# A block product in place of four seventh products, and a new order of products, in a Strassen-like matmul with RMS norm

## The chip, the cores and the metric

The kernel runs on one core of one Trainium2 chip. Its metric is the device time of one execution in microseconds (us). Of the kernel before there are three runs: 220.96, 221.03 and 221.49 us, median 221.03 us. A profile of one execution belongs to it.

The engines' names below: TensorE (PE) multiplies matrices, PEld is its loading of weights; VectorE (DVE), ScalarE (ACT) and GpSimd (POOL) work on elements; SyncE (SP) and POOL issue DMA transfers.

## The reference

```python
def reference(a, b, gamma, eps):           # all float32; a, b: 2048 x 2048
    x = np.matmul(a, b)
    rms = np.sqrt(np.mean(x ** 2, axis=-1, keepdims=True) + eps)
    return (gamma * x / rms).astype(np.float32)
```

Each output row needs the whole row of `x` for its root mean square before it can be scaled and stored.

## The kernel before

**Tiles.** The 16 blocks of 128 rows of `a` are rows 0 to 15 here. `b` stays in SBUF as bfloat16, in tiles `raw[j][kp]`: `j` is the left or right half of N (1024 columns), `kp` one of eight pairs of 128 rows of K. Rows 0 to 3 and the loading of `b` come first (lines 432 to 557). From there on two rows make a group `g`: group 2 is rows 4 and 5, group 7 rows 14 and 15. A group is worked in two halves, `j` = 0 (left) and `j` = 1 (right), in `group_half` (line 582); the last group has its own `last_group` (line 705).

**Seven products.** In a half, the 2 x 2 blocks of `a` (two rows by even and odd blocks of K) and of `b` (the two blocks of K in a pair by two runs of 512 columns) are multiplied by Strassen's scheme: seven products, numbered 1 to 7, in place of eight. One product is 8 matmuls, one for each `kp`, into one PSUM bank of 128 x 512 (`product`, line 289). The sums of `b` are made while it is loaded; products 2, 5, 6 and 7 read `raw` itself, and 7 reads `b_quarter(j, kp, 1, 0)`. The sums of `a` are made by `a_sums` (line 254) on VectorE, for each group during the right half of the group before. Products 3 and 4 need no sum of `a`.

**A half.** `group_half` issues products 2, 5, 1, 4, 3, 7, 6. ScalarE empties the first bank into a tile (line 597); VectorE adds the second to it (601), subtracts that from product 1 (605). Products 4 and 3 then accumulate onto the first two banks, and ScalarE copies them to the output tiles `x21` and `x12` (608, 613) and squares them for the norm (303). VectorE combines them to `x11` and `x22` (610, 615, 619, 624). Seven PSUM banks are handed out in turn by `new_bank` (line 391); a bank given again waits for its last reader.

**Work in between.** `hooks_of` (line 634) lists, for places 0 to 7 between the products, what else is issued there. In a left half (`j` = 0) these are, for the two rows of the next group: the row norm of the loaded block (line 219, ScalarE), a power-of-two factor from it (`row_factor`, VectorE), the rescaled block in float16 (line 242, ScalarE) and its transposing DMA (line 195, SP); for the rows of the group before: the root (`take_rms`, line 332) and the scaling with gamma (line 370, VectorE) and the stores (SP). In a right half they are the second row's scaling (`finish`), the sums of the next group and the loads of the rows after (`load_after`, POOL, which waits until `x22` of the left half is written). Squares of the last two tiles of a half are put off to the next half's start (`last_squares`, line 573).

**What sets the order.** The kernel schedules by hand (`tc.manual_schedule()`): each engine's instructions run in the order in which the code issues them, and what connects engines are waits for the data or for a buffer to be free. Output tiles are eight `x_slot` buffers of 128 x 1024, four to a group; blocks of `a` are loaded into two `a32` buffers.

Of the kernel before, what the change touches and what calls it, by code (L numbers as in the profile page):

```python
# [9 lines left out]
BF16 = mybir.dt.bfloat16  # L10
# [7 lines left out]
def kernel(  # L18
# [61 lines left out]
    def a16_slot(mb):  # L80
        if mb == HB:
            return gamma_sb[:, 0:HALF].bitcast(FP16)
        flat = head_at.rearrange("p t r m -> p (t r m)").bitcast(FP16)
        return flat[:, (2 + mb % 2) * K:(3 + mb % 2) * K]

    s_sum = {s: consts.tile([P, KP, P], FP16, name=f"s_{s}") for s in (1, 2, 5, 6, 7)}

    def at(mb):
        return (at_even, at_odd)[(mb // 2) % 2][:, mb % 2]
# [159 lines left out]
        return at(2 * g + r)[:, c::2, :]  # L249

    def sum_of(g, s):
        return s_sum[s].bitcast(BF16) if g < G0 else s_sum[s]

    def a_sums(g, which, lo=0, hi=KP):
        a11, a12, a21, a22 = (quarter(g, r, c) for r in range(2) for c in range(2))
        terms = {1: (a11, a22, ALU.add), 2: (a21, a22, ALU.add), 5: (a11, a12, ALU.add),
                 6: (a21, a11, ALU.subtract), 7: (a12, a22, ALU.subtract)}
        for s in which:
            x, y, op = terms[s]
            nc.vector.tensor_tensor(out=sum_of(g, s)[:, lo:hi, :], in0=x[:, lo:hi, :],  # L260
                                    in1=y[:, lo:hi, :], op=op)
# [32 lines left out]


    x_half = {}
    n_x = [0]

    def square(mb, src):
        c = n_sq[mb]  # L300
# [5 lines left out]
    def square_half(mb, h):  # L306
# [3 lines left out]
        nc.scalar.activation(out=sq, in_=x_tile(mb, h), func=ACTF.Square,  # L310
                             scale=inv_sqrt_n, accum_out=msq[mb][:, c:c + 1])

    def x_tile(mb, h):


        if (mb, h) not in x_half:
            n = n_x[0]
            n_x[0] += 1
            if n < 8:
                slot = n  # L320
            else:
                g = n // 4
                slot = ((0, 4, 1, 5), (0, 1, 4, 5))[g // 2 % 2 == 0][n % 4] + 2 * (g % 2)
            x_half[mb, h] = x_slot[slot]
        return x_half[mb, h]

    def x_chunk(mb, c):
# [219 lines left out]
    nc.scalar.copy(out=x12, in_=pair[5])  # L547
    p6 = new_bank()
    product(PAIR, 1, 6, p6, within={5 + g: [lambda g=g: turn(HB + 1, g)] for g in range(2)})
    a_sums(G0, (5,))  # L550
    for g in range(2):
        take_transposed(HB + 1, g, turned[HB + 1, g], nc.vector.tensor_copy)
    square_half(0, 1)
    square_half(1, 1)
    a_sums(G0, (2,))
    take_rms(0)
    a_sums(G0, (1,))

    def pair_sub():
        nc.vector.tensor_tensor(out=x22, in0=pair[1], in1=x22, op=ALU.subtract)  # L560
# [21 lines left out]
    def group_half(g, j, hooks):  # L582
        ra, rb = 2 * g, 2 * g + 1
        c1, c2 = 2 * j, 2 * j + 1

        def at_hook(n):
            for work in hooks.get(n, ()):
                work()

        x11, x12, x21, x22 = (x_chunk(ra, c1), x_chunk(ra, c2), x_chunk(rb, c1), x_chunk(rb, c2))  # L590
        first = (g, j) == (G0, 0)
        c, t = spare if first else (x22, x22)
        at_hook(0)
        p2, p5 = new_bank(), new_bank()
        one, two = ((5, p5), (2, p2)) if first else ((2, p2), (5, p5))
        product(g, j, *one)
        nc.scalar.copy(out=c, in_=one[1])  # L597
        last_squares()
        at_hook(1)
        product(g, j, *two)  # L600
        nc.vector.tensor_tensor(out=t, in0=two[1], in1=c, op=ALU.add)
        at_hook(2)
        p1 = new_bank()
        product(g, j, 1, p1)
        nc.vector.tensor_tensor(out=t, in0=p1, in1=t, op=ALU.subtract)
        at_hook(3)
        product(g, j, 4, p2, start=False)
        nc.scalar.copy(out=x21, in_=p2)
        square(rb, x21)
        nc.vector.tensor_tensor(out=x11, in0=t, in1=x21, op=ALU.add)  # L610
        at_hook(4)
        product(g, j, 3, p5, start=False)
        nc.scalar.copy(out=x12, in_=p5)  # L613
        square(ra, x12)
        nc.vector.tensor_tensor(out=t, in0=t, in1=x12, op=ALU.add)  # L615
        at_hook(5)
        p7 = new_bank()
        product(g, j, 7, p7)
        nc.vector.tensor_tensor(out=x11, in0=p7, in1=x11, op=ALU.add)
        late.append((ra, x11))  # L620
        at_hook(6)
        p6 = new_bank()
        product(g, j, 6, p6)
        nc.vector.tensor_tensor(out=x22, in0=p6, in1=t, op=ALU.add)  # L624
        late.append((rb, x22))
        at_hook(7)

    def load_after(g, mb):

# [4 lines left out]
    def hooks_of(g, j):  # L634


        hooks = {n: [] for n in range(8)}
        nxt = 2 * g + 2

        def hook(n, work, *args):  # L640
            hooks[n].append(lambda: work(*args))

        def apply(mb):
            row_apply(mb)
            transpose_dma(mb)

        more = g + 1 < NG
        if j == 0:
            if g == G0:
                hook(0, finish, 0, (1,))  # L650
                hook(1, row_norm, nxt)
                hook(1, take_rms, 1)
                hook(2, pair_sub)
                hook(2, row_factor, nxt)
                hook(2, apply, nxt)
                hook(2, row_norm, nxt + 1)
                hook(2, pair_sums)
                hook(2, a_sums, g, (7, 6))
                hook(2, finish, 0, (0,))
                hook(2, finish, 1, (1,))  # L660
                hook(2, row_factor, nxt + 1)
                hook(2, pair_ends)
                hook(2, scale, 1, (0,))
                hook(4, apply, nxt + 1)
                hook(4, store, 1, (0,))
                hook(7, late.insert, 0, (r2, None))
            else:
                done = [2 * g - 2, 2 * g - 1]
                if g == G0 + 1:
                    done.insert(0, r3)  # L670
                else:
                    hook(1, row_norm, nxt)
                for mb in done:
                    hook(1, take_rms, mb)
                hook(2, row_factor, nxt)
                hook(2, apply, nxt)
                if g == G0 + 1:
                    hook(2, finish, r3)
                hook(2, row_norm, nxt + 1)
                hook(3, scale, 2 * g - 2)  # L680
                hook(3, row_factor, nxt + 1)
                hook(4, apply, nxt + 1)
                hook(4, store, 2 * g - 2)
        else:
            if g == G0:
                hook(1, take_rms, r2)
                hook(1, square_half, r3, 1)
                hook(2, finish, r2, (1, 0))
            else:
                hook(2, finish, 2 * g - 1)  # L690
            if more:
                hook(3, a_sums, g + 1, (2, 5, 1))
                hook(6, a_sums, g + 1, (7,))
                hook(7, a_sums, g + 1, (6,))
            if g + 2 < NG:
                hook(0, load_after, g, nxt + 2)
                if g == G0:
                    hook(2, wait_for, x_slot[HB + r2][:, 0:1])
                    hook(2, load_block, nxt + 3)
                    hook(5, row_norm, nxt + 2)  # L700
                else:
                    hook(0, load_block, nxt + 3)
        return hooks

    def last_group():
# [33 lines left out]

        p4 = []  # L740
        for j in range(2):
            p5, p1 = new_bank(), new_bank()
            p4.append(new_bank())
            product(g, j, 5, p5)
            nc.scalar.copy(out=t[j], in_=p5)
            last_squares()
            product(g, j, 1, p1)
            add(t[j], p1, t[j], ALU.subtract)
            if j == 0:
                finish(2 * g - 2)  # L750
            product(g, j, 4, p4[j])
            nc.scalar.copy(out=x21[j], in_=p4[j])
            add(x11[j], t[j], x21[j])
            if j == 0:
                finish(2 * g - 1)
            product(g, j, 3, p5, start=False)
            nc.scalar.copy(out=x12[j], in_=p5)
            square(ra, x12[j])
            add(t[j], x11[j], x12[j])
            p7 = new_bank()  # L760
            product(g, j, 7, p7)
            add(x11[j], p7, x11[j])
            square(ra, x11[j])
            if j == 0:
                product(g, j, 2, p4[j], start=False)
                nc.scalar.copy(out=x21[j], in_=p4[j])
                square(rb, x21[j])
                seed = p7
                add(seed, t[j], x21[j], ALU.subtract)
                pre_a = partial(ra)  # L770
                add(xa, xa, gam_left, ALU.mult)
                add(x21[j], x21[j], gam[0], ALU.mult)
        rms_a = root(msq[ra][:, NCH - 1:NCH], plus(pre_a, ra, 2))
        product(g, 1, 2, p4[1], start=False)
        halves = [slice(0, CH // 2), slice(CH // 2, CH)]
        half = [bank[:, 0:CH // 2] for bank in (p1, p7)]
        for bank, col in zip(half, halves):
            add(bank, t[1][:, col], p4[1][:, col], ALU.subtract)
        r_a = inverse(rms_a)
# [75 lines left out]
```

## Time and profile before

| what | us |
|---|---|
| median of three runs | 221.03 |
| span of the profiled execution (first to last instruction) | 219.1 |
| TensorE busy | 209.2 |
| VectorE busy | 165.9 |
| ScalarE busy | 127.0 |
| GpSimd busy | 36.4 |
| end of the last matmul in the span | 212.23 |

The span is what the profile shows of one execution; the device time also holds what lies around it. Busy time counts an engine's own work, not its waits. A matmul of 512 columns is listed with 379 ns, but matmuls overlap: in a row they start about 216 ns apart. The same holds in a smaller way for VectorE and ScalarE: an instruction's listed duration is somewhat longer than the distance to the next one's start.

Where the prediction speaks of windows, these are stretches of the span with the busy time of PE, PEld, DVE, ACT and POOL in this order, then the granted clock of TensorE, the busy share of the DMA engines and GB/s.

### The profile page before, as it was taken

Reading aid. Unit: us, or ns where it says so; the run is one execution under the profiler, and the core shown is the slowest. Engines: PE = TensorE matmul, PEld = TensorE weight load, DVE = VectorE, ACT = ScalarE, POOL = GpSimd, SP = SyncE. Lnnn points to the kernel's source line nnn. Section 1 sums busy time; section 2 is a strip of 40 time slices with the busy share of each in tenths; the row PEclk is TensorE's granted clock in tenths of the full one; section 3 lists DMA queues with packets and bytes.
Section 4 is the critical chain, followed back from the end, with each engine's and each line's share of the span. In section 5 each row is a group of like instructions: output and inputs, shape, how many; then the busy total and the mean of one; then the engine's idle time right before and its main releaser. Section 6 shows DMA issues by size and latency. Waiting matters only on the chain.

```text
span 219.1 us, 3041 instructions
## 1 busy us (share of the span) xinstructions
PE 209.2 (95%) x1032; PEld 97.7 (45%) x1032; DVE 165.9 (76%) x326; ACT 127.0 (58%) x263; POOL 36.4 (17%) x75
## 2 busy tenths in 40 slices
PE   7799999999999999999999999999999999999970
PEld 3344544444455444444444444444444444444440
DVE  1128899999989998969696639946795759787771
ACT  2110002930599898588945996289747996334471
POOL 7554443433020002200110002000200000000040
PEclk9999999999999999999999999999999999999997
DMA  7999999999929698946799149955699259145045
GB/s 156 168 202 206 204 206 209 212 208 228 407 77 330 243 276 218 349 188 165 212 320 399 64 88 271 350 244 96 160 298 400 37 106 361 79 167 219 1 170 215
DMA packets 36720, 46.60 MB, mean 213 GB/s; under 512 B 22240, under 2 KB 26336, under 8 KB 35424
## 3 DMA queue, kind: packets, MB, share of 16 engines
q0 software_dynamic: 10608, 23.86, 44.1%
q1 hardware_dynamic: 25824, 22.29, 33.7%
q10 hardware_dynamic: 272, 0.26, 0.3%
q8 instruction: 8, 0.13, 0.2%
q14 instruction: 8, 0.07, 0.1%
HBM read 34.60 MB, written 16.78 MB: 234 GB/s over the span
## 4 chain that ended last, share of the span: by engine, by line
PE 92%; DMA 3%; ACT 1%; POOL 1%; issue 1%; DVE 0%; ACTq 0%; POOLq 0%
PE acc L285 71%; PE acc L388 16%; DMA early<-in_a_dram 3%; PE tbank L419 2%; PE tbank L168 2%; PE acc L800 1%; POOL b L102 0%; PE acc L185 0%; PE tbank L185 0%; ACT a L738 0%; DVE head_at L173 0%; ACTq L850 0%; ACT sq L803 0%; ACT rms L352 0%; POOL t_left masks.py:199 0%
## 5 line engine op out<-in xcount | busy, mean ns | idle before, releaser
L285 PE MATMUL acc<-b,s 128*128 128x512 bf16 x408 | 93.3, 379 | 0.0
L285 PEld LDWEIGHTS <-s 128*128 128x128 f16 (+1 forms) x512 | 50.0, 98 | 59.6 <-DVE s L260 0.2
L388 PE MATMUL acc<-b,head_at 128*128 128x512 bf16 x176 | 43.0, 379 | 1.2 <-DMA b<-in_b_dram 0.8
L303 ACT ACTIVATE sq<-x 128x512 bf16<-128x512 f32 x53 | 33.4, 630 | 6.9 <-DVE x L731 3.0
L370 DVE SCALAR_TENSOR_TENSOR x<-x,r,gamma_sb 128x1024 f32<-128x1024 f32 x28 | 34.9, 1282 | 0.7
L219 ACT ACTIVATE sq<-a 128x1024 bf16<-128x1024 f32 x24 | 25.3, 1054 | 3.2 <-DMA a<-in_a_dram 2.5
L388 PEld LDWEIGHTS <-head_at 128*128 128x128 bf16 x176 | 16.9, 97 | 20.4 <-issue 1.3
L242 ACT ACTIVATE head_at<-a,s 128x2048 f16<-128x2048 f32 x10 | 20.0, 1996 | 3.3 <-DVE s L229 3.3
L102 POOL DMA_DIRECT2D b<-in_b_dram x32 | 17.2, 541 | 20.6 <-DMA b<-in_b_dram 14.2
L430 ACT COPY x<-acc 128x512 f32<-128x512 f32 x5 | 2.9, 582 | 24.6 <-PE acc L388 24.6
L285 PEld LDWEIGHTS <-head_at 128*128 128x128 f16 (+1 forms) x112 | 10.9, 98 | 13.2
L285 PE MATMUL acc<-early,head_at 128*128 128x512 bf16 x64 | 14.5, 379 | 0.0
L285 PEld LDWEIGHTS <-at_even 128*128 128x128 f16 x96 | 9.4, 98 | 11.3
L285 PE MATMUL acc<-early,s 128*128 128x512 bf16 x56 | 14.2, 379 | 0.0
L260 DVE TENSOR_TENSOR s<-head_at 128x1024 f16<-128x1024 f16 (+5 forms) x22 | 13.4, 635 | 0.1
L615 DVE TENSOR_TENSOR x<-x,x 128x512 f32<-128x512 f32 x9 | 6.2, 693 | 8.8 <-ACT x L613 8.3
L127 POOL COPY pace<-x 128x1 f32<-128x1 f32 x4 | 1.7, 413 | 66.2 <-DVE x L624 64.9
L597 ACT COPY x<-acc 128x512 f32<-128x512 f32 x9 | 5.2, 573 | 11.5 <-PE acc L285 11.5
L173 DVE COPY head_at<-tbank 128x1024 bf16<-128x1024 bf16 x7 | 4.8, 692 | 8.6 <-PE tbank L168 8.5
L285 PE MATMUL acc<-t_left,s 128*128 128x512 bf16 x48 | 11.3, 379 | 0.0
L783 POOL TENSOR_SCALAR x<-x,r 128x512 f32<-128x512 f32 x1 | 2.7, 2657 | 51.2 <-DVE r L346 51.2
L276 DVE TENSOR_TENSOR b<-b 128x1024 bf16<-128x1024 bf16 x16 | 10.8, 686 | 0.2
(112 smaller groups left out, 238.0 us busy)
## 6 DMA issues: line engine op xcount, KB each, us to landing
out_dram<-x SPq DMA_DIRECT2D x29, 512.0 KB, 3.7
a<-in_a_dram POOLq DMA_DIRECT2D x10, 1024.0 KB, 9.0
b<-in_b_dram POOLq DMA_DIRECT2D x32, 256.0 KB, 10.0
a<-in_a_dram POOLq DMA_DIRECT2D x4, 512.0 KB, 9.8
early<-in_a_dram POOLq DMA_DIRECT2D x7, 256.0 KB, 10.0
gamma_sb<-in_gamma_dram POOLq DMA_DIRECT2D x2, 512.0 KB, 8.4
out_dram<-x SPq DMA_DIRECT2D x3, 256.0 KB, 2.6
out_dram<-a SPq DMA_DIRECT2D x1, 768.0 KB, 3.3
```

What stands on the lines that cost most here:

```text
L102: nc.gpsimd.dma_start(out=raw[j][kp][:, t, :], in_=b[lo:lo + P, j * HALF:(j + 1) * HALF])
L173: nc.vector.tensor_copy(out=head_at[:, 2 * kp:2 * kp + 2, :, :], in_=view)
L219: nc.scalar.activation(out=junk, in_=a32[mb][:, h * HALF:(h + 1) * HALF], func=ACTF.Square, scale=2.0 ** -8, accum_out=n2[:, h:h + 1])
L242: nc.scalar.activation(out=a16[mb], in_=a32.pop(mb), func=ACTF.Copy, scale=factor.pop(mb))
L260: nc.vector.tensor_tensor(out=sum_of(g, s)[:, lo:hi, :], in0=x[:, lo:hi, :], in1=y[:, lo:hi, :], op=op)
L276: nc.vector.tensor_tensor(out=flat[:, 1:3, :], in0=flat[:, 1:3, :], in1=flat[:, 0::3, :], op=ALU.add)
L285: nc.tensor.matmul(bank, lhsT[:, kp, :], rhs, start=(start and kp == 0), stop=(kp == KP - 1), skip_group_check=not start)
L303: nc.scalar.activation(out=sq[:, 0:CH], in_=src, func=ACTF.Square, scale=inv_sqrt_n, accum_out=msq[mb][:, c:c + 1])
L370: nc.vector.scalar_tensor_tensor(out=x, in0=x, scalar=inverse_of[mb], in1=gamma_sb[:, h * HALF:(h + 1) * HALF], op0=ALU.mult, op1=ALU.mult)
L388: nc.tensor.matmul(bank, head_at[:, kt, r, :], head_rhs(c, kt), start=(kt == 0), stop=(kt == KT - 1))
L597: nc.scalar.copy(out=c, in_=one[1])
L615: nc.vector.tensor_tensor(out=t, in0=t, in1=x12, op=ALU.add)
```

## The change

Two things change for the groups from 2 on.

*Order.* Products are issued as 3, 4, 1, 5, 2, 7, 6; 5 accumulates onto 3's bank and 2 onto 4's. The sums are rewritten to fit. In groups 4 to 7 product 7 is left out of the half.

*Product 7 of two groups at once.* Groups 4 and 5, and groups 6 and 7, are pairs. The product 7 of both groups and both halves is a 2 x 2 block product: `y` (the two groups' sum 7, each cut in two along K) times `z` (`b_quarter(j, kp, 1, 0)`, two halves of N by two halves of `kp`). It is made by seven block products of 4 matmuls each, 28 matmuls, where four times 8 stood. `z_sums` makes differences of `z` (VectorE, 128 x 512 bf16), 12 of them once during group 4 and 4 in each pair; `y_sums` makes four sums of `y` in each pair (VectorE, 128 x 512 f16). `sevenths` issues the parts: `one` ahead of product 6 of the first group's right half, `two` behind it, `three` behind product 3 of the second group's left half. ScalarE copies a bank into another bank (`seed`), so that a part accumulates onto both. The results go into `x11` of both groups; the second group's `x11` is written before that group starts.

With it go: the second group's sums 1, 5, 2, 6 are made in its own left half, since the block product uses those buffers; the sums of `b` and `a` share buffers (`z_store`, `s_both`, `y_sum`); the blocks of `a` from row 6 on are rescaled to float16 in place in their `a32` buffer; the output tiles' slots are given by a table; the second group of a pair has its rows finished in reversed order.

```diff
+    s_both = consts.tile([P, 2, KP, P], FP16, name="s_both")
+    s_sum |= {2: s_both[:, 0], 5: s_both[:, 1]}
...
+        return a32[mb].bitcast(FP16)[:, 0:K]
...
         at_hook(0)
+        p3, p4 = new_bank(), new_bank()
+        product(g, j, 3, p3)
+        nc.scalar.copy(out=c, in_=p3)
         last_squares()
         at_hook(1)
+        product(g, j, 4, p4)
+        add(t, p4, c)
         at_hook(2)
         p1 = new_bank()
         product(g, j, 1, p1)
+        add(t, p1, t)
+        if second:
+            add(x11, x11, t)
         at_hook(3)
+        product(g, j, 5, p3, start=False)
+        nc.scalar.copy(out=x12, in_=p3)
+        square(ra, x12)
+        add(x11, x11 if second else t, x12, ALU.subtract)
+        if second:
+            late.append((ra, x11))
+        at_hook(4)
+        product(g, j, 2, p4, start=False)
+        nc.scalar.copy(out=x21, in_=p4)
         square(rb, x21)
+        add(t, t, x21, ALU.subtract)
         at_hook(5)
+        if g < FIRST_PAIR:
+            p7 = new_bank()
+            product(g, j, 7, p7)
+            add(x11, p7, x11)
+            late.append((ra, x11))
         at_hook(6)
         p6 = new_bank()
         product(g, j, 6, p6)
+        add(x22, p6, t)
...
+    def z_sums(k, which):
+        for n, (out, x, y) in enumerate((
+                (z_sum[3][:, k, :], z22[k], z12[k]), (z12[k], z12[k], z11[k]),
+                (z_sum[2][:, k, :], z22[k], z12[k]),
+                (z_sum[4][:, k, :], z21[k], z_sum[2][:, k, :]))):
+            if n not in which:
+                continue
+            nc.vector.tensor_tensor(out=out, in0=x, in1=y, op=ALU.subtract)
...
+        for s in which:
+            out, x, y, op = {3: (y_sum[3], y11, y21, ALU.subtract),
+                             1: (y21, y21, y22, ALU.add),
+                             2: (y_sum[2], y21, y11, ALU.subtract),
+                             4: (y_sum[4], y12, y_sum[2], ALU.subtract)}[s]
...
+        def one():
+            part(1, 1, y11, lambda k: z11[k], start=True)
+            part(7, 7, y_sum[3], lambda k: z_sum[3][:, k, :], start=True)
+            seed(2, 1)
+            nc.scalar.copy(out=to21, in_=b[7])
+        def two():
+            part(6, 2, y_sum[2], lambda k: z_sum[2][:, k, :])
+            part(2, 1, y12, lambda k: z21[k])
+            seed(3, 2)
+            add(to11, 1)
+            square(2 * g, to11)
+            part(5, 3, y21, lambda k: z12[k])
+            nc.vector.tensor_tensor(out=to22, in0=b[3], in1=to21, op=ALU.add)
+            part(4, 2, y22, lambda k: z_sum[4][:, k, :])
+            add(to21, 2)
+        def three():
+            part(3, 3, y_sum[4], lambda k: z22[k])
+            add(to12, 3)
+            square(2 * g, to12)
...
                 done = [2 * g - 2, 2 * g - 1]
+                if second_of_pair(g):
+                    done.reverse()
+                    hook(1, a_sums, g, (1, 5))
+                    hook(1, steps[g - 1][2])
+                    hook(2, a_sums, g, (2, 6))
...
+                if g == FIRST_PAIR:
+                    hook(5, z_sums, 0, (0, 1, 2))
+                    hook(7, z_sums, 1, (0, 1, 2))
...
+            if first_of_pair(g):
+                steps[g] = sevenths(g)
+                if g == FIRST_PAIR:
+                    hook(1, z_sums, 2, (0, 1, 2))
+                    hook(4, z_sums, 3, (0, 1, 2))
+                hook(3, a_sums, g + 1, (7,))
+                hook(4, y_sums, g, (3, 1, 2))
+                hook(6, steps[g][0])
+                hook(6, z_sums, 0, (3,))
+                hook(6, z_sums, 1, (3,))
+                hook(7, z_sums, 2, (3,))
+                hook(7, z_sums, 3, (3,))
+                hook(7, y_sums, g, (4,))
+                hook(7, steps[g][1])
+            elif more:
+                hook(3, a_sums, g + 1, (1,))
+                hook(5, a_sums, g + 1, (5, 2))
                 hook(6, a_sums, g + 1, (7,))
                 hook(7, a_sums, g + 1, (6,))
```

`last_group` is changed in the same way: products 3, 4, 1, 5, 2 in the left half with `three` behind its product 3, its sums made there, row 13 finished after product 4 and row 12 after product 1; in the right half 3, 4, 1, 5, then 2 and the two products 6 as before.

## The prediction

> **What bounds the kernel now.** I read the chain of waits first, then busy time by half of a row group, then the timeline around one such half. A half is one group of two row blocks against one half of N: 56 matmuls.
>
> ```profile
> core 0 of [0], span 219.1 us
> ...
> 66.73 143.74 PE acc L285 x666
> 210.47 1.76 PE acc L800 x16
> ```
>
> In the chain TensorE runs from 66.73 us to 212.23 us without one piece in between: 143.74 / 666 = 0.2158 us per matmul. A product of 8 is 1.727 us, a half of 7 products 12.09 us. So fewer matmuls pay, if TensorE still never waits. The windows of group 4's left and right half (columns: length, then busy time by engine) show what spare the others have:
>
> ```profile
> 115.35:127.43 12.08, 12.08 (x58) 5.48 (x56) 7.49 (x18) 9.55 (x19) 0.00 (x0) 1.00 0.65 229
> 127.43:139.52 12.09, 12.09 (x58) 5.49 (x57) 9.61 (x17) 8.47 (x18) 1.24 (x3) 1.00 0.78 200
> ```
>
> VectorE (third) has 17.1 us of work in 24.2, ScalarE (fourth) 18.0. The averages hide where the work stands, so the timeline (start, duration, engine, line):
>
> ```profile
> 117.27 0.59 ACT L597 COPY x<-acc 128x512 f32<-128x512 f32 x1 [3.84 <-PE acc L285]
> ...
> 130.11 0.56 ACT L613 COPY x<-acc 128x512 f32<-128x512 f32 x1
> 130.70 0.63 ACT L303 ACTIVATE sq<-x 128x512 bf16<-128x512 f32 x1
> 130.70 0.69 DVE L615 TENSOR_TENSOR x<-x,x 128x512 f32<-128x512 f32 x1 [2.20 <-ACT x L613]
> 130.88 1.89 PE L285 MATMUL acc<-early,s 128*128 128x512 bf16 x8
> ...
> 131.33 0.57 ACT L597 COPY x<-acc 128x512 f32<-128x512 f32 x1
> 131.91 0.68 DVE L624 TENSOR_TENSOR x<-acc,x 128x512 f32<-128x512 f32 x1
> ...
> 132.51 0.68 DVE L601 TENSOR_TENSOR x<-acc,x 128x512 f32<-128x512 f32 x1
> ...
> 133.37 2.48 DVE L370 SCALAR_TENSOR_TENSOR x<-x,r,gamma_sb 128x1024 f32<-128x1024 f32 x2
> ```
>
> Two things are to be seen. Group 4's left half ends on TensorE at 127.43, but its last sum (L624) is made at 131.91: ScalarE's chain from the first copy of one half (117.27) to the end of the first copy of the next (131.90) is 14.63 us long, because it squares and rescales the next two A blocks in between. And the third product after it starts accumulating into that copy's bank at 130.88 + 1.73 = 132.61: the spare is 0.71 us. A lag that is invisible today is nearly used up.
>
> **The change, part by part.** T4 to T7 are the starts of groups 4 to 7 on TensorE (T4 = 115.35 in this trace).
>
> Matmuls: product 7 goes from four groups and both halves, 64, and 2 x 28 come: -8 x 0.2158 = -1.73 us. [...]
>
> Order 3, 4, 1, 5, 2, 7, 6: I put this at nothing in groups 2 and 3. The first bank is still emptied by ScalarE, the second read by VectorE, and two products still lie between each read and the accumulation into that bank; the cover is 0.71 us as above, and without it the wait is TensorE's.
>
> Work added: VectorE makes 12 + 2 x 4 differences of B quarters (z), 8 sums of A (y) and 4 more additions. The nearest row for z is a difference of the same shape and type made earlier in the kernel:
>
> ```profile
> 42.13 1.09 DVE L271 TENSOR_TENSOR t_left<-b 128x512 bf16<-128x512 bf16 x3
> ```
>
> Three in a row took 1.09 us and one takes 0.42, so they start 0.34 us apart. For y (128x512 f16) no row exists: between 0.34 (L271) and 0.60 (L260, twice the elements, three starting 0.60 apart from 112.11); I take 0.34, same count and width as L271. The f32 additions of 512 columns also start 0.60 apart, two scalings (L370) take 2.40 until the next may start, the reciprocal ahead 0.19. ScalarE gets three copies per pair, two of them from bank to bank: between 0.38 (square of half a bank, L803) and 0.70 (L731, VectorE into a bank), I take 0.59 as for L597. They lie beside the four-matmul parts; the tight one, between parts 6 and 5, has part 2 (0.86 us) as cover against 0.19 (a product's end at 117.08 to its copy's start) + 0.59: nothing, at the upper bound under 0.1.
>
> What matters is where the added work stands: the rows above follow the code's order on each engine, waits included, so I lay the new order out with the old steps.
>
> *Group 4, right half.* Without product 7 the left half is 6 products, so the right one starts at T4 + 10.36 and part 7 of the block product is due at 10.36 + 5 x 1.727 + 0.86 = T4 + 19.86. It needs y3, and y3 stands behind this list on VectorE, which begins when ScalarE's copy of x21 is there. That copy keeps its place in ScalarE's chain, nothing before it is taken away: 130.70 - 115.35 = T4 + 15.35. Then: t minus x21 0.60; z of k = 0, 1.01; x22 0.60; z of k = 1 and 2, 2.01; p4 + c 0.60; row 7's scaling 2.59; p1 + t 0.60; sum 7 of group 5, 0.60; x11 0.60; z of k = 3, 1.01; y3 with its latency 0.42. Sum 10.64, so T4 + 25.99: TensorE stands 6.1 us, in three places. Product 5 waits for the copy c (cover 0.71 less 1.73: 1.0), product 2 for p4 + c, which z of k = 1 and 2 stand before (about 2), part 7 for y3 (about 3.1). With hand-over 6.2. If y costs 0.60 it is 0.3 more.
>
> *Group 5.* Its sums move to its own left half: 1 and 5 before product 4, needed after part 3 and product 4, T5 + 4.3; they are made by T5 + 2.1. 2 and 6 follow p4 + c, done near T5 + 5.7, needed at 7.8. No wait. Left half 11.22 us with part 3. ScalarE's chain: first copy at T5 + 1.92, plus 14.63, plus 0.35, since its square of row 8 waits for VectorE to add part 3 (made by T5 + 3.5, ScalarE free at 3.15): 16.90, against product 5 of the right half at 11.22 + 5.18 = T5 + 16.40: 0.5 us.
>
> *Group 6.* As group 4 without the twelve z: 15.35 + 0.60 + 0.60 + 0.60 + 2.59 + 0.60 + 0.60 + 0.60 + 0.42 = T6 + 21.96. VectorE enters group 6 late from group 5's right half (it ends its last f32 sum about 0.5 us after ScalarE could square it): 0.4 more, bounds 0 and 0.8. 22.36 + 0.1 less 19.86: 2.6 us, product 5 taking 1.5 of it.
>
> *Group 7.* Left half: VectorE must do one addition and two sums, the addition of part 3 (T7 + 3.4), p4 + c (5.1), two sums (6.3), row 13's root and scaling 0.62 + 2.40 (rows 192.18 to 195.19 of this trace), two additions, row 12's 0.62 + 2.40, x11 0.60: T7 + 14.1. ScalarE then squares x11, copies and squares x21, and copies c: + 0.7 + 0.59 + 0.63 + 0.59 = 16.7, against product 5 of the right half at 9.50 + 5.18 = T7 + 14.68: 2.0. The two waits that follow (product 2 for p4 + c, the last matmuls for their seeded banks) 0.5, and the end, which now has product 7's 1.73 us less to hide the last squares in, 0.3. Together 2.8.
>
> Blocks of A rescaled in place: a load must wait for the transposing DMA of the block before. Those landed 4.3 us after issue, the second at 134.57 where its buffer's load was issued at 133.80: 0.8 us later, on POOL's queue, with nothing but loads behind it. That load landed at 145.33 and was first read at 148.61: nothing, and up to 1 us on ScalarE's chain if transfers crowd. The block product writes two tiles of group 5 early, one of them row 7's, whose store took from 134.68 to 144.55; the write comes near T4 + 31 = 146.4, and the sum that TensorE needs behind it has 2 to 3 us of cover: nothing.
>
> Sum: 6.2 + 0.5 + 2.6 + 2.8 = 12.1 of waits, less 1.73: + 10.4. The profiled execution has a span of 219.1 and about 1.9 around it, against a median of 221.03; 221.03 + 10.4 = 231.4 us, span about 229.5.
>
> **The rivals.** *It does what the matmul count says*: 221.03 - 1.73 = 219.3, faster. It decides from the point where VectorE and ScalarE get no later than TensorE's 10.36 us halves. For it: the unbroken chain, and VectorE's idle 4.6 us in each left half. Against it: that idle time lies before x21's copy, and the z stand behind that copy.
>
> *The z find cover*: if the twelve z ahead of y3 cost nothing, group 4 falls to 25.99 - 4.03 - 19.86 = 2.1, sum 8.0: 227.3. For it: idle time exists. Against it: the written order.
>
> *The clock falls too.* The granted clock is 1.00 in every window up to 216, 3.8 us after the last matmul, and 0.50 from 217 on; the gaps I forecast are at most 3.1 us each. For it: they come close. Against it: that they stay shorter. A halved clock over the product of 8 that follows a gap costs 1.73 us; after the two gaps at part 7, 3.5: 234.9.
>
> [...]
>
> **How the numbers follow.** Forecast 0.72, clock or late transfers on top 0.10, z covered 0.10, all covered 0.05, gain and waits cancelling 0.03. The measurement tells 0.3% from nothing. So faster 0.05, same 0.03, slower 0.92. The forecast's own range, with hand-overs of 0.1 more or less at nine waits, y at its upper bound and half of group 6's 0.8, is 229.5 to 233.5; to the two slower rivals 227.3 to 235.
>
> **What would show it.** In the changed profile TensorE should wait in group 4's right half for ScalarE's copy, for VectorE's p4 + c and for y3 (3 us, 1 us in group 6), the right half lasting near 20 us, not 12; 1024 matmuls in all; the last matmul 10 us later. A TensorE run still unbroken to the end would make all this wrong; waits in group 5's left half for its sums would mean that I placed them wrongly; a clock under 1.00 before the end, the third rival.

## The result, and the profile after

The changed kernel takes 240.81 us (median of 4 runs, 239.44 to 242.31), the kernel before 221.26 us beside it: a ratio of 1.088 (95% interval 1.084 to 1.093). It is slower, as forecast, but by 19.6 us where I forecast 10.4, and outside my range. The profiled execution is the slowest of the four (242.31 us); its span is 240.5 us.

The view of TensorE's waits of the changed kernel (what it waited for: us in total, times, the longest):

```profile
PE acc L308 <- ACT x L620: 5.0, 5, 1.6
PE acc L691 <- DVE s L679: 4.5, 2, 3.3
PE acc L308 <- DVE x L615: 2.6, 1, 2.6
PE acc L408 <- DMA b<-in_b_dram: 2.4, 1, 2.4
PE acc L308 <- ACT x L868: 2.2, 1, 2.2
```

The unbroken run of 666 matmuls is gone. The first three rows are the three waits that I had named: L620 is ScalarE's copy c of product 3's bank, L679 a sum y (here y3, which part 7 of the block product reads), L615 a sum of output tiles, here p4 + c (product 4's bank and that copy). L868 is the copy c in the last group. But the first row has five places and I had three (groups 4, 5 and 6); two are in groups 2 and 3. "L408 <- DMA" is in the start-up and belongs to this execution: the first matmul of group 2 starts at 69.15 us here, at 66.6 to 67.4 us in eleven of the twelve profiled kernels below (at 70.7 us in the twelfth, the one with both repairs, after a wait of 2.8 us at the same line). Behind that wait the granted clock of the changed kernel is 0.50 from 7.98 to 11.39 us; so it is in the twelfth, from 7.53 to 14.35 us, and in the start-up of no other.

Where the span's 21.4 us more came from, by the starts of the halves on TensorE (us more than before; the forecast is that of the prediction with the matmuls added or removed in each group):

| stretch | forecast | profile |
|---|---|---|
| start-up, to the first matmul of group 2 | 0 | +2.15 |
| groups 2 and 3 | 0 | +3.74 |
| group 4 | +7.9 | +10.45 |
| group 5 | -2.1 | -1.98 |
| group 6 | +4.3 | +4.88 |
| group 7, to the last matmul's start | -0.1 | 0.0 |
| after it | +0.3 | +2.1 |

Groups 5 to 7 came out as worked, within 0.6 us each. The error lies in the start-up, in groups 2 and 3, in group 4 and at the end. Group 4's halves in windows, columns as in the prediction:

```profile
121.23:131.59 10.36, 10.36 (x49) 4.68 (x48) 7.67 (x17) 7.85 (x16) 0.00 (x0) 1.00 0.63 250
131.59:155.86 24.27, 17.50 (x74) 7.30 (x72) 17.95 (x39) 11.68 (x24) 1.30 (x3) 0.93 0.70 216
```

The left half is six products without a gap (10.36 us). The right half has 72 matmuls, 15.54 us at 0.2158, and lasts 24.27; its mean clock is 0.93. The timeline (T4 = 121.23):

```profile
135.99 0.56 ACT L640 COPY x<-acc 128x512 f32<-128x512 f32 x1
...
136.59 0.69 DVE L615 TENSOR_TENSOR x<-x 128x512 f32<-128x512 f32 x1 [2.20 <-ACT x L640]
137.19 0.42 DVE L666 TENSOR_TENSOR head_at<-b,b 128x512 bf16<-128x512 bf16 x1
137.22 0.56 ACT L620 COPY x<-acc 128x512 f32<-128x512 f32 x1
137.65 0.42 DVE L666 TENSOR_TENSOR b<-b,b 128x512 bf16<-128x512 bf16 x1
137.83 1.89 PE L308 MATMUL acc<-b,s_both 128*128 128x512 bf16 x8 [0.90 <-ACT x L620]
138.10 0.42 DVE L666 TENSOR_TENSOR head_at<-b,b 128x512 bf16<-128x512 bf16 x1
138.45 0.68 DVE L615 TENSOR_TENSOR x<-acc,x 128x512 f32<-128x512 f32 x1
...
139.96 0.76 DVE L666 TENSOR_TENSOR head_at<-b,b 128x512 bf16<-128x512 bf16 x2
...
142.29 1.89 PE L308 MATMUL acc<-b,s_both 128*128 128x512 bf16 x8 [2.57 <-DVE x L615]
...
147.87 0.42 DVE L679 TENSOR_TENSOR s<-s,t_first 128x512 f16<-128x512 f16 x1
148.34 1.89 PE L691 MATMUL acc<-head_at,s 128*128 128x512 bf16 x4 [3.30 <-DVE s L679]
```

TensorE's three gaps are 1.06, 2.74 and 3.46 us long from where the next matmul was due (the brackets leave out the tail of the last one). The copy of x21 ends at T4 + 15.32; I had 15.35. From there to y3's end VectorE takes 11.74 us; I had 10.64. The z (L666) are most of that: within the three of one k each starts 0.455 us after the one before, not 0.335. In "x2" stand the last of one three and the first of the next, which share no data, and there the step is the 0.34 of L271.

In group 2 the view to look at is ScalarE:

```profile
79.08 1.57 SPq L396 DMA_DIRECT2D out_dram<-x  x2
...
81.64 3.61 PE L308 MATMUL acc<-early,at_even 128*128 128x512 bf16 x16 [0.24 <-DVE x L586]
82.63 0.59 ACT L633 COPY x<-acc 128x512 f32<-128x512 f32 x1 [3.12 <-DMA out_dram<-x]
...
87.61 3.62 PE L308 MATMUL acc<-b,s_both 128*128 128x512 bf16 x15 [0.63 <-ACT x L620]
```

The copy into x12 (L633) stands idle for 3.12 us until a store has left the tile it writes. The next A block is rescaled later, the copy c too (L620), and product 5 waits.

### The profile page after: what moved, and what is told of

Read it like the earlier page. It is cut to its first block, busy times and chain, and to the rows that moved or that the text cites. A ratio compares the mean times of both kernels' runs of the same rounds, so it can differ in the third digit from the quotient of the medians.

```text
span 240.5 us, 3070 instructions
## 1 busy us (share of the span) xinstructions
PE 212.2 (88%) x1024; PEld 97.4 (40%) x1024; DVE 179.6 (75%) x358; ACT 128.8 (54%) x267; POOL 36.3 (15%) x75
## 5 line engine op out<-in xcount | busy, mean ns | idle before, releaser
L308 PE MATMUL acc<-b,s_both 128*128 128x512 bf16 x208 | 49.9, 379 | 10.4 <-ACT x L620 5.0
L408 PE MATMUL acc<-b,head_at 128*128 128x512 bf16 x176 | 44.5, 390 | 2.4 <-DMA b<-in_b_dram 2.4
L308 PEld LDWEIGHTS <-s_both 128*128 128x128 f16 (+1 forms) x208 | 20.3, 97 | 36.8 <-issue 13.4
L308 PEld LDWEIGHTS <-s 128*128 128x128 f16 (+1 forms) x240 | 23.6, 99 | 28.3 <-issue 1.4
L308 PE MATMUL acc<-b,s 128*128 128x512 bf16 x136 | 32.6, 385 | 0.0
L408 PEld LDWEIGHTS <-head_at 128*128 128x128 bf16 x176 | 17.3, 100 | 22.7 <-issue 4.4
L615 DVE TENSOR_TENSOR x<-acc,x 128x512 f32<-128x512 f32 x31 | 20.9, 685 | 4.0 <-PE acc L308 3.8
L263 ACT ACTIVATE a<-a,s 128x2048 f16<-128x2048 f32 x10 | 20.0, 1996 | 3.3 <-DVE s L250 3.3
L450 ACT COPY x<-acc 128x512 f32<-128x512 f32 x5 | 2.9, 581 | 24.6 <-PE acc L408 24.6
L615 DVE TENSOR_TENSOR x<-x 128x512 f32<-128x512 f32 x11 | 7.5, 688 | 8.5 <-ACT x L640 8.3
L308 PE MATMUL acc<-t_left,head_at 128*128 128x512 bf16 x48 | 11.2, 379 | 0.0
```

What stands on the lines that cost most here:

```text
L263: nc.scalar.activation(out=a16[mb], in_=a32.pop(mb), func=ACTF.Copy, scale=factor.pop(mb))
L308: nc.tensor.matmul(bank, lhsT[:, kp, :], rhs, start=(start and kp == 0), stop=(kp == KP - 1), skip_group_check=not start)
L408: nc.tensor.matmul(bank, head_at[:, kt, r, :], head_rhs(c, kt), start=(kt == 0), stop=(kt == KT - 1))
L450: copy(out=x_chunk(*g), in_=banks[g])
L615: nc.vector.tensor_tensor(out=out, in0=in0, in1=in1, op=op)
```

## The experiments

### The order alone

With the pairs switched off all groups make product 7 themselves, in the new order; the last group's product 7 follows its product 2 (left out below).

```diff
-    FIRST_PAIR = 4
+    FIRST_PAIR = 16
...
+            product(g, j, 7, other)
+            add(x11[j], other, x11[j])
```

> The change's order of products alone: all groups keep their own product 7, so 1032 matmuls, and no block product is made. The prediction as it stands on record: nothing, 221.0 to 221.5 us, TensorE unbroken from group 2 on. Theory 1 (formed on the changed kernel's trace): the new order writes x12 of group 2 first, into the tile whose store went out last, and the wait of 3.1 us on ScalarE runs through groups 2 and 3: gaps on TensorE of about 3.7 us there, 224.5 to 225.5 us, nothing lost from group 4 on. Theory 2: those gaps belong to the block product's other edits; then 221 here.

Measured 227.27 us, ratio 1.030 (1.027 to 1.033). In groups 2 and 3 gaps at the same five places as in the changed kernel (0.62, 0.79, 1.70, 0.46, 0.29 us). Three more, 2.4 us together, stand in group 6, where the table of slots is made for an order of finishing that this kernel does not have. So the order, or what was changed with it, does cost something before the block product begins.

### The table of output tiles

Row 4's left tile was given slot 0, which holds row 0's left half, of that row's two halves the one stored last (issued at 79.08 us in the changed kernel, the right half at 73.10). Before, x21 was written first and x12 later; the new order writes x12 first. The edit swaps the two slots in group 2 and, so that each stays free in time, in group 4.

```diff
-    for n, slots in enumerate(((0, 4, 1, 5), (2, 6, 3, 7), (0, 1, 4, 5), (2, 3, 6, 7),
+    for n, slots in enumerate(((4, 0, 1, 5), (2, 6, 3, 7), (4, 1, 0, 5), (2, 3, 6, 7),
```

> The changed kernel with another table of output tiles for groups 2 and 4 (row 4's left tile and row 5's left tile swapped), so that what is written first goes where the older store was. Theory 1: the gaps of groups 2 and 3 go, 3.7 us less, about 237 us; group 4's right half stays at 24 us. Theory 2: they come from loads that wait for the transposing DMA, since blocks of A are rescaled in place; then they stay and the time is 240.8.

Measured 236.84 us, ratio 1.072 (1.066 to 1.079); against the changed kernel's 1.088 this is 3.5 us less. The copy no longer waits (timeline of this variant):

```profile
76.59 1.58 SPq L396 DMA_DIRECT2D out_dram<-x  x2
76.93 0.57 ACT L633 COPY x<-acc 128x512 f32<-128x512 f32 x1
```

Groups 2 and 3 have no gap, group 4's three gaps are the same to 0.01 us (1.06, 2.74, 3.46); behind them the clock was at half for 6.83 us here, for 3.41 in the changed kernel. The same edit on the order alone:

> The order alone (seven products in every group, no block product) with the tiles of group 2 swapped as well. Theory 1: no gap from group 2 on, the time of the kernel before, 221.0 to 221.5. Theory 2 (the order itself costs, by ScalarE's later first copies): 224 or more as in the order alone.

Measured 223.00 us, ratio 1.010 (1.008 to 1.011). Groups 2 and 3 are clean; two gaps of 0.46 and 1.50 us are left, in group 6, where the table is made for the reversed finishing that this variant lacks and the copy c waits for a store:

```profile
168.37 0.59 ACT L620 COPY x<-acc 128x512 f32<-128x512 f32 x1 [6.65 <-DMA out_dram<-x]
```

So the order alone was run once more with the kernel before's slots in groups 4, 6 and 7 and group 2's swap:

```diff
-    for n, slots in enumerate(((4, 0, 1, 5), (2, 6, 3, 7), (4, 1, 0, 5), (2, 3, 6, 7),
-                               (5, 1, 4, 0), (2, 3, 6, 7))):
+    for n, slots in enumerate(((4, 0, 1, 5), (2, 6, 3, 7), (0, 1, 4, 5), (2, 3, 6, 7),
+                               (0, 4, 1, 5), (2, 6, 3, 7))):
```

> The order alone, seven products in every group, with the tiles of groups 6 and 7 as in the kernel before and those of group 2 swapped. The table that the change brought for group 6 fits rows finished in reversed order; without the reversal ScalarE's first copy of group 6 waited 6.65 us for a store. Theory 1: the order of products costs nothing by itself: 220.9 to 221.5 us and no gap after group 2 starts. Theory 2: something in the order stays, 222 to 223.

Measured 221.47 us over 10 runs, ratio 0.998 (0.994 to 1.002). Its chain of waits is unbroken again:

```profile
core 0 of [0], span 219.0 us
...
66.58 143.75 PE acc L308 x666
```

The order of products and the blocks of A rescaled in place cost nothing; the slot of one tile did.

### The twelve z moved

The twelve z ahead of y3 go into VectorE's idle time in group 4's left half, ahead of and between the two row factors.

```diff
-                    hook(5, z_sums, 0, (0, 1, 2))
-                    hook(7, z_sums, 1, (0, 1, 2))
+                    hook(2, z_sums, 0, (0, 1, 2))
+                    hook(2, z_sums, 1, (0, 1, 2))
...
+                    hook(3, z_sums, 2, (0, 1, 2))
...
+                    hook(4, z_sums, 3, (0, 1, 2))
...
-                    hook(1, z_sums, 2, (0, 1, 2))
-                    hook(4, z_sums, 3, (0, 1, 2))
```

> The changed kernel with the twelve differences of B made earlier, in group 4's left half, where VectorE waits for ScalarE. Theory 1: group 4's right half falls from 24.3 us to that of group 6 (18.7) or a little less, no gap over 3 us is left and so the clock stays full there: 5 to 6 us less, 235 us. Theory 2: VectorE has too much work over the whole pair, and the work moved only moves the wait: group 4 as a whole keeps 34 us, 240.8.

Measured 236.13 us, ratio 1.069 (1.067 to 1.071): 4.3 us less than the changed kernel, where I expected 5 to 6. Group 4's right half falls from 24.27 to 18.49 us; what is left there is a gap of 1.57 us for the copy c, now made 0.5 us later (the rescaling of the A block waits 0.92 us for its row factor, which stands behind z; 0.42 in the changed kernel), and one of 1.37 us for y3. The gap for p4 + c is gone and so is the fall of the clock in this half. In group 5 the gaps grow from 0.61 us to 0.53 and 1.39; the first is a wait that was hidden before (timeline):

```profile
148.98 0.69 DVE L714 TENSOR_TENSOR x<-acc,x 128x512 f32<-128x512 f32 x1 [2.35 <-DMA out_dram<-x]
...
149.73 0.81 PE L691 MATMUL acc<-b,s 128*128 128x512 bf16 x3 [0.37 <-DVE x L714]
```

L714 is the block product's early write into a tile of group 5. In the changed kernel it comes 34.0 us after group 4's start and waits for no store; here it comes at 30.4, having waited 2.35 us for row 7's. With both repairs together:

> The changed kernel with both repairs, the tiles of group 2 swapped and the twelve differences of B moved into VectorE's waits. Theory 1 (separate costs that add): 3.9 and 4.7 us less than the changed kernel, 240.8 - 8.6 = 232 us, with no gap before group 4's right half and the gaps for ScalarE's first copy, for y3 and in the last group still there. Theory 2 (one lag that finds another place): 235 or more.

Measured 232.6 us, ratio 1.048 (1.042 to 1.054): the two add up within the interval (3.5 + 4.3 of 19.6 us would leave 11.8; 10.7 are left). Groups 2 and 3 are free of gaps.

### Product 6 earlier

To test whether the remaining waits are a matter of how much TensorE work lies ahead of them, in groups 4 to 6 product 6 was put ahead of 5, part 1 of the block product ahead of product 2, and part 7 left where it was. The rest is the kernel with both repairs; group 5's sum 6 is made before its sum 2.

```diff
         at_hook(3)
+        if g >= FIRST_PAIR:
+            p6 = new_bank()
+            product(g, j, 6, p6)
         product(g, j, 5, p3, start=False)
...
-                hook(6, steps[g][0])
+                hook(4, steps[g][0])
+                hook(6, steps[g][3])
```

> As the version with both repairs, and in groups 4 to 7 (but the last) product 6 is issued before product 5, part 1 of the block product before product 2 and part 7 behind it. That gives 1.73 us more between ScalarE's first copy and the product that accumulates onto its bank, and as much more before y3 is needed: the cover that product 7 took along. Theory 1 (the lost cover is what stalls TensorE): the gaps of 1 to 1.8 us for the copy and of 1.4 us for y3 go, about 6 to 7 us less: 225 to 226 us. Theory 2 (VectorE and ScalarE are short of time as such): the gaps stay in sum, 230 or more.

Measured 229.69 us, ratio 1.036 (1.032 to 1.041): 2.6 us less than with the repairs alone, where I expected 6 to 7. The copy's gaps shrank, from 1.56 to nothing in group 4 and from 1.78 to 0.78 in group 6. The gaps for y3, expected to go too, stayed at 1.20 and 1.37: in group 4 y3 is made 22.7 us after the group's start with and without the move, and the two gaps together, 2.94 us before, fell by the 1.73 us of one product, which could be spent only once. And the wait for row 7's store grew in group 5, from 0.98 to 2.26 us. In the last variant I also moved row 12's scaling behind x11 in the last group:

```diff
-            if j == 0:
-                finish(2 * g - 2)
             product(g, j, 5, p3, start=False)
...
             square(ra, x11[j])
+            if j == 0:
+                finish(2 * g - 2)
```

> As the one before, and in the last group row 12 is scaled after the sum that ScalarE squares, not before it. Theory 1: the gap of 2.3 us for the last right half's first copy goes, 2 to 2.5 us less than the one before: 223 us, still above the kernel before by what the end loses. Theory 2 (the scaling's 2.6 us of VectorE are missing later anyway): the same time as the one before.

Measured 228.70 us, ratio 1.032 (1.027 to 1.037), and not the 223 expected: the last group's gap fell only from 2.32 to 2.00 us. Product 5 no longer waits for the copy c there; instead product 2 waits for p4 + c, since the scaling's 2.4 us now stand ahead of that sum on VectorE. The wait for the store in group 5, in this variant's timeline:

```profile
145.62 0.69 DVE L720 TENSOR_TENSOR x<-acc,x 128x512 f32<-128x512 f32 x1 [3.11 <-DMA out_dram<-x]
...
146.37 1.02 PE L695 MATMUL acc<-b,s 128*128 128x512 bf16 x4 [1.93 <-DVE x L720]
```

This variant's sum closes: gaps of 1.20, 2.09, 0.65, 0.78, 1.37 and 2.00 us are 8.1, less 1.73 for the matmuls, 0.8 more after the last matmul: +7.2, and its span is 7.3 above that of before. No version of the block product that I made beats the kernel before.

### When the clock falls

In the changed kernel the clock was halved after the gap of 3.46 us, not after that of 2.74; in the variants with z or slots moved it was halved after one of 2.32 us in the last group. Two readings: only a gap nearly as long as that of 3.46 us does it (theory 1; the 2.32 us speak against it), or a window fixed in time counts (theory 2). The kernel before was given extra VectorE work, on a tile that nothing uses, ahead of L601 in four right halves, which makes gaps of chosen length. Each of these four kernels ran once.

```diff
+        for _ in range({3: 4, 4: 5, 5: 6, 6: 7}.get(g, 0) if j == 1 else 0):
+            nc.vector.tensor_tensor(out=spare[1], in0=spare[1], in1=spare[1], op=ALU.max)
```

> The kernel before, with 4, 5, 6 and 7 extra maxima of VectorE on a tile that nothing uses, ahead of the sum of p4 and p5 (L601) in the right halves of groups 3, 4, 5 and 6: nothing of the output changes. Each maximum should take about 0.69 us and the first 1.1 us of them should be covered, so TensorE should stand still for about 1.7, 2.4, 3.0 and 3.7 us, 10.8 us in all. The longest of these decide between two theories of the clock in the changed kernel. [...] Theory 2 (gaps from about 2.3 us on do it when they lie badly to some fixed window): falls after two or three gaps, also after 2.4 or 3.0 us, 235 to 237 us.

> The same with 7, 6, 5 and 4 maxima in groups 3, 4, 5 and 6, so that the same gaps come in the reverse order and lie elsewhere in time. [...] Theory 2: falls after gaps of 2.4 or 3.0 us too, and not the same number of them as in the run beside it, since the gaps lie differently to the window.

The first: 237.94 us (theory 2 had 235 to 237), gaps of 2.35, 2.41, 3.14 and 3.87 us, falls with those of 2.35, 3.14 and 3.87. The second: 235.64 us, gaps of 4.54, 3.14, 2.41 and 1.69 us, one fall, after 4.54. Falls come with gaps of 2.35 and 3.14 us, and the same length of 3.14 us brings a fall in one and none in the other: theory 1 is out. Then four gaps of one kind each, with 5 and 6 maxima:

> The kernel before with 5 extra maxima of VectorE ahead of L601 in the right halves of groups 3 to 6; nothing of the output changes. Four gaps of about 2.4 us on TensorE, 9.6 us together, so 230.5 us before any fall of the clock, and 1.7 us more for each fall. Theory 2, sharpened by the runs so far: time is cut into windows of 3.41 us, the clock is halved for the window after one in which TensorE stood still for more than about 2.03 us in all (falls followed windows with 2.09 us or more, none followed 1.97 or less). Then every fall here starts a whole multiple of 3.41 us before the fall at the end of the kernel, and exactly those gaps bring one of which more than 2.03 us lie in one window: for a gap of 2.4 us about half of them, so 232 to 236 us. [...]

> The same with 6 maxima: four gaps of about 3.1 us, 12.5 us together, 233.4 us before any fall. Theory 2: two to four falls, at multiples of 3.41 us before the last, and only a gap that a window's edge cuts into two pieces of which neither is over 2.03 us brings none; 237 to 240 us. [...]

231.84 us with gaps of 1.44, 2.42, 2.41 and 2.41 (the first was shorter than meant) and 234.84 us with 2.74, 3.14, 3.14 and 3.14; one fall in each, 61.44 and 88.75 us before that at the end, 18.0 and 26.0 times 3.413. Both times lie below what theory 2 had, 232 to 236 and 237 to 240 us. Now windows of 3.41 us counted back from there (TensorE's busy time follows the length; the third number from the end is the granted clock). First the kernel with 5 maxima:

```profile
161.63:165.04 3.41, 1.31 (x7) 0.49 (x5) 3.27 (x6) 1.69 (x5) 1.10 (x3) 1.00 1.11 310
165.04:168.46 3.42, 3.27 (x8) 1.13 (x8) 3.32 (x6) 0.00 (x0) 0.00 (x0) 0.50 0.96 343
```

The kernel with 6 maxima:

```profile
109.22:112.63 3.41, 1.41 (x7) 0.54 (x6) 3.27 (x6) 1.38 (x4) 0.81 (x2) 1.00 1.07 308
136.52:139.93 3.41, 1.02 (x5) 0.39 (x4) 3.27 (x6) 1.39 (x4) 0.84 (x2) 1.00 1.06 303
139.93:143.34 3.41, 2.82 (x7) 0.99 (x7) 3.31 (x5) 0.00 (x0) 0.00 (x0) 0.50 0.99 384
167.24:170.65 3.41, 1.45 (x7) 0.68 (x7) 3.27 (x6) 0.37 (x2) 0.00 (x0) 1.00 1.02 305
```

The gaps of 3.14 us in the first two of the four kernels: the window that a fall follows (4 to 7 maxima) and the one that none follows (7 to 4):

```profile
164.24:167.65 3.41, 1.02 (x5) 0.39 (x4) 3.27 (x6) 1.40 (x4) 0.85 (x2) 1.00 1.07 305
140.01:143.42 3.41, 1.56 (x7) 0.62 (x7) 3.24 (x6) 1.98 (x5) 1.40 (x3) 1.00 1.12 312
```

And the changed kernel:

```profile
141.11:144.52 3.41, 2.23 (x11) 1.04 (x11) 3.27 (x6) 0.37 (x2) 0.45 (x1) 1.00 0.80 223
144.52:147.93 3.41, 0.52 (x3) 0.03 (x1) 3.34 (x8) 1.49 (x4) 0.00 (x0) 1.00 1.01 384
147.93:151.34 3.41, 3.00 (x8) 1.07 (x9) 2.48 (x7) 0.58 (x1) 0.00 (x0) 0.50 0.98 404
```

In these, windows with 1.31, 1.02 or 0.52 us of TensorE work are followed by one at half clock, windows at full clock with 1.41 or more are not. (One window that was itself at half clock held more and was followed by another: 2.24 us in the variant with slots moved, 140.96 to 144.37 us.) My 2.03 us of standing still was a little low: the window at 109.22 held 2.16 us of it, counted from where the next matmul was due, and brought no fall. So the falls of these runs agree with theory 2; of the four gaps with 6 maxima one brought a fall, where I had expected two to four.

## Why the prediction was right and wrong

**What TensorE waits for in groups 4 to 7: right.** Copy c, p4 + c and y3 were named, with 1.0, 2 and 3.1 us in group 4; they were 1.06, 2.74 and 3.46. Group 5: 0.5 forecast, 0.61. Group 6: 1.5 and 1.1, found 1.77 and 1.38. Group 7: 2.0 and 0.5, found 2.32 and 0.30. The matmuls saved are 8, as counted, and every half without a gap lasts what its matmuls take.

**"Order 3, 4, 1, 5, 2, 7, 6: I put this at nothing in groups 2 and 3": wrong, 3.7 us, the largest part.** I asked which bank is read when, and that was right: with fitting slots the order costs nothing (ratio 0.998). I did not ask which output tile is written first, and whose store must have left it. The diff's table of slots kept row 4's left tile, now written first, on the later stored of the two slots that the half uses.

**"For y ... I take 0.34" and 0.34 for z from L271: the mis-sized term, 1.0 us in group 4.** Twelve z took 5.0 us (1.25 + 2.50 + 1.25), not 4.03. The row I used (three in 1.09 us) holds sums none of which writes what another reads; z's do, and start 0.455 us apart. The y start 0.46 us apart, too; only the first of them stands on the path to part 7.

**"The clock falls too": a rival that came in on top, 1.5 us in group 4.** My gap of 3.1 us at part 7 became 3.46 by the z, and the clock was halved from 147.93 to 151.34 us, over matmuls that started at 148.34. I gave it 0.10 and thought of single gaps. The runs show falls with gaps of 2.32 us too, in the last group of four variants.

**"The end ... 0.3": 2.1 us.** Two things make it. The last squares, and with them the last store's issue, come 3.54 us after the last matmul's start, 2.76 before and in the three variants with the order alone: 0.78 us that product 7 used to hide. It is the same where the last group ran at full clock (the last variant with product 6 earlier), and is gone in the four variants where the clock fell in the last group and gave ScalarE time (16 matmuls there took 5.30 us in the first variant with product 6 earlier; 16 at full clock take 3.61 in the changed kernel, at 81.64). And the last store lands late (DMA issues on the changed kernel's profile page; the last number is us from issue to landing):

```profile
out_dram<-a SPq DMA_DIRECT2D x1, 768.0 KB, 4.7
```

It was 3.3 before. It was 4.6 or 4.7 in the three variants with slots, z or both moved, and 3.3 in the two with product 6 earlier, whose last group issues the same stores; why is open.

**"The block product writes two tiles ... early ... nothing": right for this kernel, by its lateness alone.** Once z or products were moved, that wait was next, 0.5 to 2.3 us.

The rivals on the other side (z covered: 227.3; all covered: 219.3) did not come. The z do find cover in the left half, worth 4.3 us, but only if they are issued there.

Of the 11.0 us between my 10.4 and the profile's 21.4, groups 2 and 3 are 3.7, the start-up of this execution 2.15, the end 1.8, the clock in group 4 1.5, z 1.0 and the small excesses of groups 5 to 7 0.8. The start-up's share is not in most executions; the median is 1.5 us below this run.

## What to carry to other kernels

When the order of products changes, follow every buffer that the order touches, output tiles and their stores as well as PSUM banks: the tile that is written first must be the one whose store left first. Eight matmuls (1.7 us) were saved for 32 more VectorE instructions, most of them in halves where the spare in front of the first of these waits was 0.71 us. Where the engines beside TensorE have no slack at the spot, count there, not in the average. And a moved instruction uncovers the next wait: sum the gaps that stand behind the one you remove before you expect its full length back.

## What the runs showed of the hardware

Two things were new to me. The granted clock was halved in steps of one length: a fall between matmuls lasted 3.41 us (147.93 to 151.34 us in the changed kernel) or twice that (140.96 to 147.78 us with slots moved), and in a trace with several falls each started a whole number of such lengths after another. In the changed kernel they start at 7.98, 147.93 and 236.67 us, 41.0 and 26.0 times 3.413 us apart; in the kernel with gaps of 2.35 to 3.87 us it is 3.413 us times 16.0, 9.0 and 10.0. Windows fixed in time would give this; no view shows the windows themselves. Counted in such windows from group 2 on, in all traces of this case, falls between matmuls at full clock followed 1.36 us of TensorE work and less (40% of 3.41), and none followed 1.41 and more. So whether a gap of 2.3 us brought a fall depended on where it lay: that of 2.32 us in the last group brought one in four variants and none in the changed kernel's profile. A fall cost 1.5 us in group 4 of the changed kernel and 1.69 over those 16 matmuls of the last group (5.30 us for 3.61). No gap of 2.0 us or less brought one.

And VectorE: 128x512 bf16 sums and differences started 0.335 us apart where none writes what another reads (L271 of the kernel before, three in 1.09 us, one in 0.42), and differences 0.455 us apart where one reads or overwrites what the one before wrote or read (L666 of the changed kernel, at 137.19, 137.65 and 138.10 us). I would price a chain of such short dependent operations by the second.
